# Four products of the feed-forward step's pairs 4 and 5, made at the kernel's start from the transposed input

## The chip, the cores and the metric

One core of a Trainium2 chip runs the whole block. TensorE (PE) multiplies, VectorE (DVE), ScalarE (ACT) and GpSimd (POOL) work element by element, SyncE (SP) issues most loads and stores. The metric is device time in microseconds, the median of several executions.

## The reference

```python
h = h + 0.5 * swiglu(rms_norm(h, ffn1_norm[l]), ffn1_w1[l], ffn1_w3[l], ffn1_w2[l])
...
def swiglu(x, w1, w3, w2):
    return (jax.nn.silu(x @ w1) * (x @ w3)) @ w2
```

The change lies in the first of these lines, the block's first step, with 1024 tokens of 1024 features, 2816 hidden features, all float32. `rms_norm` scales each token by one number and each feature by its gain. Attention, pooling, a merge and a second such step follow.

## The kernel before

Every float32 product is made of three products of a high and a low part (`three`), accumulated in PSUM. The matrix x is cut into 2 x 2 blocks of 512 tokens by 512 features, and a pair j of two 128-wide slices of hidden features (2j and 2j+1) is made with seven block products instead of eight, for w1 (`A`) and for w3 (`B`). `ORDER` is their order; product 1 is block b11 of x by weight block a11, product 2 is b21 by a12, added in the same bank. One product is 12 matmuls of 128x512. `Pair.a_out` and `Pair.b_out` take each bank apart: product 1 is copied as u2, product 2 is read from the bank where 1 + 2 stand, the others are added.

`begin_up1` is the kernel's start, written by hand in the order in which each engine gets its instructions; each engine works through its own queue in that order. It loads eight blocks of 128 token rows (`load_rows`, L882), between them the first weights (L76), from SyncE's queue. ScalarE squares a row block with a sum (L274), VectorE and GpSimd make the inverse root (L278, L279), VectorE scales by it and by the gain (L285), TensorE turns the block (L407, four transposes), ScalarE rounds the turned block to the high part (L408), VectorE subtracts for the low part (L411), ScalarE keeps the turned block (L415). The gain as a row is made by spreading the gain's column over 128 columns (L920), turning it (L926) and copying it from PSUM (L942, L960). `keep_on` (L916) puts filler matmuls of ones into TensorE's queue. `entry` makes products 1 and 2 of pairs 0 to 2 one after the other (`operand`: weights split at L319 and L322; `product`: L331; `out`: L567 and L591) while the later row blocks are being turned. Its first four use b11 and are products 1 of pairs 0 and 1; the fifth is product 2 of pair 0 and needs all four row blocks of b21. After that `up` runs the rest of the pairs; pairs 3 to 9 do so one after the other, all products of `A`, then all of `B`. Weights come through seven buffers (`raw`), a pair's first rows lie in one of three (`tmp`).

## Time and profile before

| | us |
|---|---|
| median of 3 executions | 1892.59 |
| lowest, highest | 1892.32, 1893.02 |
| profiled execution: its time | 1892.07 |
| profiled execution: its span on the core | 1890.2 |

A row of the timeline gives start, duration, engine, line, operation and tiles (numbers left out), the count of merged instructions, and in brackets the idle time before with what ended it. A row of stretches gives busy time and the number of instructions of each engine, then the granted clock, the share of the transfer engines and GB/s. "PEld" is TensorE's loading of weights, which overlaps with its matmuls.

### The profile page before, as it was taken

The numbers are of one execution on the slowest core, as the hardware profiler recorded it, in microseconds if no ns is written. First come the engines' busy times: TensorE is split into PE (matmuls) and PEld (weight loads), VectorE is DVE, ScalarE is ACT, GpSimd is POOL, SyncE is SP. The second block draws the span as 40 slices with busy tenths as digits, with TensorE's granted clock in tenths as the row PEclk, the third lists the DMA queues.
The fourth block names the chain that finished last, engine by engine and source line by source line (L and its number), as shares of the span: only waits on it lengthen the run. The fifth ranks groups of instructions, "written<-read, shape, count | busy, mean of one in ns | idle before, by whom it ended". The sixth has DMA issues, their size and how long they took to land.

```text
span 1890.2 us, 24694 instructions
## 1 busy us (share of the span) xinstructions
PE 1879.9 (99%) x8822; PEld 1561.9 (83%) x8822; DVE 1331.9 (70%) x1975; ACT 772.8 (41%) x1394; POOL 712.2 (38%) x533
## 2 busy tenths in 40 slices
PE   9999999999999999999999999999999999999998
PEld 8888888888888888888888888888888888888887
DVE  6776556657786777557885896887665566577867
ACT  7323333333334553334445772363333323334344
POOL 5433333331223254444555357543333333312221
PEclk9999999999999999999999999999999999999999
DMA  5154223436566526765668968744332223454654
GB/s 191 60 198 166 84 89 106 139 111 216 170 224 210 183 84 210 236 219 188 224 236 314 322 224 289 270 153 149 140 127 103 84 102 118 137 189 162 226 197 145
DMA packets 144019, 330.79 MB, mean 175 GB/s; under 512 B 17560, under 2 KB 39064, under 8 KB 142360
## 3 DMA queue, kind: packets, MB, share of 16 engines
q1 hardware_dynamic: 140152, 318.36, 48.6%
q10 hardware_dynamic: 3744, 10.85, 1.6%
q8 instruction: 70, 1.15, 0.3%
q14 instruction: 53, 0.43, 0.1%
HBM read 229.61 MB, written 99.55 MB: 174 GB/s over the span
## 4 chain that ended last, share of the span: by engine, by line
PE 57%; DVE 2%; ACT 1%; DMA 1%; issue 0%; POOL 0%; ACTq 0%; DVEq 0%; SPq 0%
PE u_mixm L331 15%; PE d_f L815 11%; PE wo L2028 4%; PE yp L1770 1%; PE u_f20b L331 1%; PE u_f21a L331 1%; PE u_f210b L331 1%; PE u_f210a L331 1%; PE u_f29b L331 1%; PE u_f29a L331 1%; PE u_f28a L331 1%; PE u_f27b L331 1%; PE u_f27a L331 1%; PE u_f26b L331 1%; PE u_f26a L331 1%; PE u_f25b L331 1%
## 5 line engine op out<-in xcount | busy, mean ns | idle before, releaser
L815 PE MATMUL d_f<-bhi_f,ahi_f 128*128 128x512 f32 x616 | 240.2, 390 | 0.0
L815 PE MATMUL d_f<-bhi_f,alo_f 128*128 128x512 f32 x616 | 239.7, 389 | 0.0
L815 PE MATMUL d_f<-blo_f,ahi_f 128*128 128x512 f32 x616 | 239.6, 389 | 0.0
L772 POOL TENSOR_TENSOR alo_f<-g_f,ahi_f 128x512 fp32r<-128x512 f32 x60 | 85.9, 1448 | 270.0 <-ACT ahi_f L768 270.0
L331 PE MATMUL u_mixm<-xhi_t_mix,wc_mixm 128*128 128x512 f32 x608 | 157.3, 391 | 0.1
L815 PEld LDWEIGHTS d_f<-bhi_f,ahi_f 128*128 128x128 f32 x616 | 115.7, 188 | 24.2 <-ACT h L415 0.5
L815 PEld LDWEIGHTS d_f<-bhi_f,alo_f 128*128 128x128 f32 x616 | 115.6, 188 | 24.2
L815 PEld LDWEIGHTS d_f<-blo_f,ahi_f 128*128 128x128 f32 x616 | 115.7, 188 | 23.7
L331 PEld LDWEIGHTS u_mixm<-xhi_t_mix,wc_mixm 128*128 128x128 f32 x608 | 113.5, 188 | 23.9 <-ACT wc_mixm L319 0.7
L331 PE MATMUL u_mixm<-xhi_b_mix,wc_mixm 128*128 128x512 f32 x456 | 120.4, 391 | 0.0
L322 POOL TENSOR_TENSOR wc_mixm<-s_mixm,wc_mixm 128x512 fp32r<-128x512 f32 x52 | 76.6, 1475 | 104.9 <-ACT wc_mixm L319 94.0
L331 PEld LDWEIGHTS u_mixm<-xhi_b_mix,wc_mixm 128*128 128x128 f32 x456 | 84.9, 188 | 17.3
L319 ACT ACTIVATE wc_mixm<-s_mixm 128x512 fp32r<-128x512 f32 x76 | 47.0, 628 | 109.4 <-DVE s_mixm L373 54.6
L768 ACT ACTIVATE ahi_f<-g_f 128x1024 fp32r<-128x1024 f32 x84 | 81.9, 975 | 3.1 <-DMA g_f<-gs_f 2.0
L331 PE MATMUL u_mixm<-xlo_t_mix,wc_mixm 128*128 128x512 f32 x304 | 81.3, 389 | 0.0
L322 POOL TENSOR_TENSOR wc_mixm<-raw,wc_mixm 128x512 fp32r<-128x512 f32 x40 | 60.2, 1505 | 40.8 <-ACT wc_mixm L319 32.4
L2028 PE MATMUL wo<-w_o,o_hi 128*128 128x512 f32 x224 | 69.3, 390 | 0.0
L768 ACT ACTIVATE bhi_f<-s_f2w 128x512 fp32r<-128x512 f32 x55 | 33.0, 628 | 86.3 <-DVE s_f2w L790 67.6
L768 ACT ACTIVATE bhi_f<-s_f1w 128x512 fp32r<-128x512 f32 x55 | 33.1, 629 | 83.4 <-DVE s_f1w L790 70.2
L331 PEld LDWEIGHTS u_mixm<-xlo_t_mix,wc_mixm 128*128 128x128 f32 x304 | 57.1, 188 | 12.0
L772 DVE TENSOR_TENSOR alo_f<-g_f,ahi_f 128x1024 fp32r<-128x1024 f32 (+1 forms) x48 | 57.6, 1200 | 7.6 <-ACT ahi_f L768 7.5
L331 PE MATMUL u_mixm<-xlo_b_mix,wc_mixm 128*128 128x512 f32 x228 | 61.0, 389 | 0.0
(1332 smaller groups left out, 4751.9 us busy)
## 6 DMA issues: line engine op xcount, KB each, us to landing
g_f<-gs_f SPq DMA_DIRECT2D x70, 512.0 KB
gs_f<-y_f SPq DMA_DIRECT2D x88, 256.0 KB
raw<-in_w2a_dram SPq DMA_DIRECT2D x35, 512.0 KB
raw<-in_w2b_dram SPq DMA_DIRECT2D x35, 512.0 KB
gs_f<-gb_f SPq DMA_DIRECT2D x46, 256.0 KB
raw<-in_w1a_dram SPq DMA_DIRECT2D x22, 512.0 KB
raw<-in_w3a_dram SPq DMA_DIRECT2D x22, 512.0 KB
raw<-in_w1b_dram SPq DMA_DIRECT2D x22, 512.0 KB
```

The source lines that it names most:

```text
L319: ac.activation(w[:, 0], src, AF.Copy)
L322: eng.tensor_tensor(w[:, 1], src, w[:, 0].bitcast(F32), op=OP.subtract)
L331: pe.matmul(p, a, b, start=(start and n == 0), stop=(n == 11), skip_group_check=not start)
L768: ac.activation(hi[:, c], src, AF.Copy)
L772: eng.tensor_tensor(lo[:, d], src[:, o], hi[:, d].bitcast(F32), op=OP.subtract)
L815: pe.matmul(self.banks[m][t], l, r, start=(first and q == 0), stop=(last and q == 2))
L1770: pe.matmul(p, a, b, start=(j == 0), stop=(j == 11))
L2028: pe.matmul(banks[m][t], l, r, start=(st == 0 and j == 0 and q == 0), stop=(st == 1 and j == 1 and q == 2))
```

## The change

Products 1 of pairs 4 and 5, for w1 and w3, are made in `begin_up1`, before x is normalised. The transposed input `x_t` (an input that both kernels have) holds b11 unscaled; four of its 128-feature slices are multiplied by the gain, which is a factor of each partition there, and split (`led_high`, `led_low`) into the space of t4. The four weight blocks are loaded (`weight`) and split (`led_split`, `led_rest`), the first two in halves. `led_run` issues the matmuls, partly for half of the slices at a time. The factor of each token, a column of the result, comes later: `means` is the row of the four inverse roots, turned from a column read with a zero step, and `led_scaled` multiplies the kept products by it and stores them to `led_dram`. In pairs 4 and 5 `fetch_a` and `fetch_b` load them as u2, product 1 is left out, and product 2 is added to u2 by VectorE.

The gain's row is turned in the same way without a spread copy; `first_scaled` reads it from PSUM. The fillers of TensorE are 7 and 2 now. Block 1's high part is made by VectorE. The fourth block of b21 is turned after the third product.

On TensorE, from the gain's transposes to the first product of pair 0 (`idle` are the fillers, `x_b11_0` to `x_b11_3` the four row blocks, `f10a1` is product 1 of pair 0), before:

```order
L926 MATMUL gain0_230<-ident_70,columns_143 128x128 x4
L926 MATMUL gain1_235<-ident_70,columns_143 128x128 x4
L916 MATMUL idle_211<-ones_71 128x128 x2
L407 MATMUL x_b11_0_252<-ident_70,x0_133 128x128 x4
L916 MATMUL idle_211<-ones_71 128x128 x2
L407 MATMUL x_b11_1_261<-ident_70,x1_134 128x128 x4
L916 MATMUL idle_211<-ones_71 128x128 x2
L407 MATMUL x_b11_2_277<-ident_70,x2_135 128x128 x4
L916 MATMUL idle_211<-ones_71 128x128 x3
L407 MATMUL x_b11_3_287<-ident_70,x3_136 128x128 x4
L916 MATMUL idle_211<-ones_71 128x128 x2
L331 MATMUL u_f10a1_300<-xhi_b11_f1_123,wc_f10a1_273 128x512 x8
```

and now, from block 0 to just before the same place (`led2` and `led3` are products 1 of pair 5; those of pair 4, `led0` and `led1`, stand ahead):

```order
L409 MATMUL x_b11_0_321<-ident_70,x0_133 128x128 x4
L1025 MATMUL u_led2_308<-xhi_t4_f1_119,wc_led2_299 128x512 x4
L1025 MATMUL u_led3_336<-xhi_t4_f1_119,wc_led3_317 128x512 x4
L409 MATMUL x_b11_1_343<-ident_70,x1_134 128x128 x4
L1025 MATMUL u_led3_336<-xlo_t4_f1_120,wc_led3_317 128x512 x4
L409 MATMUL x_b11_2_357<-ident_70,x2_135 128x128 x4
L1025 MATMUL u_led3_336<-xhi_t4_f1_119,wc_led3_317 128x512 x2
L409 MATMUL x_b11_3_369<-ident_70,x3_136 128x128 x4
L971 MATMUL means_375<-ident_70,nst_0_295 128x128
L971 MATMUL means_375<-ident_70,nst_1_302 128x128
L971 MATMUL means_375<-ident_70,nst_2_327 128x128
L971 MATMUL means_375<-ident_70,nst_3_341 128x128
```

All fillers between the blocks are gone, and the blocks' transposes stand between the new matmuls; the row after these is two more of `led3`, and then `f10a1`.

On ScalarE, from the weights of the fourth product to the weights of the fifth (`wc_f10a2`), before:

```order
L319 ACTIVATE wc_f11b1_354<-raw3_203 128x512
L408 ACTIVATE xhi_b21_f1_127<-x_b21_2_361 128x4x128
L408 ACTIVATE xhi_b21_f1_127<-x_b21_3_368 128x4x128
L591 ACTIVATE u_f102_389<-u_f10b1_336 128x512
L274 ACTIVATE columns_143,nst_5_391<-x5_138 128x1024
L415 ACTIVATE x0_133<-x_b21_0_323 128x512
L415 ACTIVATE x1_134<-x_b21_1_330 128x512
L415 ACTIVATE x2_135<-x_b21_2_361 128x512
L415 ACTIVATE x3_136<-x_b21_3_368 128x512
L319 ACTIVATE wc_f10a2_411<-raw0_195 128x512
```

and now:

```order
L320 ACTIVATE wc_f11b1_444<-raw3_216 128x512
L411 ACTIVATE xhi_b21_f1_127<-x_b21_2_451 128x4x128
L611 ACTIVATE u_f102_473<-u_f10b1_426 128x512
L411 ACTIVATE xhi_b21_f1_127<-x_b21_3_475 128x4x128
L274 ACTIVATE square2_146,nst_5_481<-x5_138 128x1024
L420 ACTIVATE x0_133<-x_b21_0_413 128x512
L420 ACTIVATE x1_134<-x_b21_1_420 128x512
L420 ACTIVATE x2_135<-x_b21_2_451 128x512
L420 ACTIVATE x3_136<-x_b21_3_475 128x512
L320 ACTIVATE wc_f10a2_501<-raw0_208 128x512
```

The fourth block's high part now follows the copy of the second product, and on TensorE its transposes have moved behind the third product:

```order
L409 MATMUL x_b21_2_451<-ident_70,x2_135 128x128 x4
L332 MATMUL u_f11a1_460<-xhi_b11_f1_123,wc_f11a1_441 128x512 x4
L332 MATMUL u_f11a1_460<-xlo_b11_f1_124,wc_f11a1_441 128x512 x4
L332 MATMUL u_f11a1_460<-xhi_b11_f1_123,wc_f11a1_441 128x512 x4
L409 MATMUL x_b21_3_475<-ident_70,x3_136 128x128 x4
L332 MATMUL u_f11b1_488<-xhi_b11_f1_123,wc_f11b1_444 128x512 x4
L332 MATMUL u_f11b1_488<-xlo_b11_f1_124,wc_f11b1_444 128x512 x4
L332 MATMUL u_f11b1_488<-xhi_b11_f1_123,wc_f11b1_444 128x512 x4
L332 MATMUL u_f10a1_385<-xhi_b21_f1_127,wc_f10a2_501 128x512 x4
```

On VectorE the scaling of block 2 (`x2_135`) stands behind the high part of block 1 and the low part of block 0:

```order
L986 SCALAR_TENSOR_TENSOR x1_134<-x1_134,nst_1_302,gain0_242 128x512
L278 TENSOR_SCALAR nst_2_327<-nst_2_327 128x1
L413 CAST xhi_b11_f1_123<-x_b11_1_343 128x4x128
L416 TENSOR_TENSOR xlo_b11_f1_124<-x_b11_0_321,xhi_b11_f1_123 128x4x128
L986 SCALAR_TENSOR_TENSOR x2_135<-x2_135,nst_2_327,gain0_242 128x512
L278 TENSOR_SCALAR nst_3_341<-nst_3_341 128x1
L986 SCALAR_TENSOR_TENSOR x3_136<-x3_136,nst_3_341,gain0_242 128x512
```

Before, it stood right behind the two small rows `nst_2` and `nst_3`.

The diff:

```diff
             x = {1: "b11", 2: "b21", 3: "b22", 4: "t4", 5: "t1", 6: "t2", 7: "t3"}[m]
             key = {1: "x", 2: "x", 5: "v", 3: "v"}.get(m, m)
-            if m not in (2, 3):
+            first = key not in self.bank
+            if first:
                 self.bank[key] = bank("mm" if key in ("x", "v") else "acc", f"u_{self.sv.name}{n}{m}")
-            self.sv.product(self.bank[key], w, x, start=m not in (2, 3))
+            self.sv.product(self.bank[key], w, x, start=first)
             if m == 3 and back:
                 raws.back(2)
             return self.bank[key]
...
+        def __init__(self, X, what, src, t, tag="acc", p=None, eng=ac):
             q = t % 4
             self.hi, self.lo = (v[:, :, q * P:(q + 1) * P] for v in X[what])
             p = self.flat = bank(tag, f"x_{what}_{t}") if p is None else p
             self.p = p.rearrange("p (k q) -> p k q", k=4)
             for k in range(4):
                 pe.transpose(self.p[:, k, :], src[:, k * P:(k + 1) * P], ident)
-            ac.activation(self.hi, self.p, AF.Copy)
+            if eng is ac:
+                ac.activation(self.hi, self.p, AF.Copy)
+            else:
+                eng.tensor_copy(self.hi, self.p)
...
+            self.led = sv.led.get(j)
+            self.order = ORDER if self.led is None else (2, *(m for m in ORDER if m not in (1, 2)))
...
+        def fetch_a(self):
+            if self.led is not None:
+                nc.sync.dma_start(self.place(0, slice(HALF, S)), self.led[0])
+
+        def fetch_b(self):
+            if self.led is not None:
+                self.u[2] = self.u2(f"{self.j}2")
+                nc.sync.dma_start(self.u[2], self.led[1])
...
             elif m == 2:
-                ac.activation(self.place(0, lows), p, AF.Silu)
+                c = self.place(0, lows)
+                if self.led is not None:
+                    ve.tensor_tensor(c, p, u2, op=OP.add)
+                    p = c
+                ac.activation(c, p, AF.Silu)
...
             q, then = then or Pair(sv, j, sums), None
-            for m in ORDER:
+            for m in q.order[:3]:
+                q.a(m)
+            q.fetch_b()
+            for m in q.order[3:]:
                 q.a(m)
             if j == NPAIR - 2:
                 between()
-            for m in ORDER[:-2]:
+            if j + 1 in sv.led:
+                then = Pair(sv, j + 1, sums)
+                then.fetch_a()
+            for m in q.order[:-2]:
                 q.b(m)
             if j == NPAIR - 2:
                 end = Pair(sv, NPAIR - 1, sums)
                 for m in ORDER[:2]:
                     end.A.operand(m)
-            for m in ORDER[-2:]:
+            for m in q.order[-2:]:
...
-    square = row("square")
-    columns_tile = tmp("columns")
-    columns = columns_tile.rearrange("p (k c) -> p k c", k=KT)
+    led_x, led_in = [], []
+    for n in range(2):
+        led_x.append(row(f"led_x{n}").rearrange("p (k c) -> p k c", k=2))
+        led_in.append(row(f"led_w{n}").rearrange("p (k c) -> p k c", k=2))
+    square = X["t1"][0][:, 0:2, :].rearrange("p k c -> p (k c)")
+    square2 = tmp("square2")
+
+    LED = (4, 5)
+    led_dram = [dram.tile([P, HALF], F32, name=f"led{q}") for q in range(4)]
...
     def load_all():
-        load_rows(0, 1, 2, 3)
+        def features(kk):
+            nc.sync.dma_start(led_x[kk], x_t[0, kk])
+
+        def weight(q):
+            nc.sync.dma_start(led_in[q // 2][:, q % 2], (w1a, w3a)[q % 2][2 * LED[q // 2]][:, LOWS])
+
+        features(0)
+        weight(0)
+        weight(1)
+        features(1)
+        load_rows(0)
+        weight(2)
+        load_rows(1)
+        weight(3)
+        load_rows(2, 3)
...
-        def widen(b):
-            k = slice(4 * b, 4 * b + 4)
-            ve.tensor_copy(columns[:, k], gain1[:, k, None].to_broadcast([P, 4, P]))
+        def spread(p, columns):
+            for k, c in enumerate(columns):
+                pe.transpose(p[:, k * P:(k + 1) * P], c.to_broadcast([P, P]), ident)
+            return p
 
         def gains(b):
-
-            p = bank("acc", f"gain{b}")
-            for k in range(4):
-                pe.transpose(p[:, k * P:(k + 1) * P], columns[:, 4 * b + k], ident)
-            return p
+            return spread(bank("acc", f"gain{b}"), [gain1[:, k:k + 1] for k in range(4 * b, 4 * b + 4)])
+
+        def gain_copy(b):
+            ac.activation(gain_row[:, (LOWS, HIGHS)[b]], g[b], AF.Copy)
...
+        def first_scaled(t):
+            ve.scalar_tensor_tensor(h[t][:, LOWS], h[t][:, LOWS], inv[t][:, 1:2], g[0], op0=OP.mult, op1=OP.mult)
+
+        xhi, xlo = X["t4"]
+        kept = [sv1.half_tile("s", f"led{q}") for q in range(4)]
+        means = sv1.half_tile("u", "means")
+        led_w, led_p = {}, {}
...
+        def led_high(k, eng=ac):
+            if eng is ac:
+                ac.activation(xhi[:, k], led_x[k // 2][:, k % 2], AF.Copy, scale=gain1[:, k:k + 1])
+            else:
+                ve.tensor_scalar(xhi[:, k], led_x[k // 2][:, k % 2], gain1[:, k:k + 1], None, op0=OP.mult)
+
+        def led_low(k):
+            ve.scalar_tensor_tensor(xlo[:, k], led_x[k // 2][:, k % 2], gain1[:, k:k + 1], xhi[:, k].bitcast(F32),
+                                    op0=OP.mult, op1=OP.subtract)
+
+        def led_split(q, c):
+            if q not in led_w:
+                led_w[q] = fp.tile([P, 2, HALF], F32R, tag="wc", bufs=4, name=f"wc_led{q}")
+            w, src = led_w[q], led_in[q // 2][:, q % 2]
+            ac.activation(w[:, 0, c], src[:, c], AF.Copy)
+
+        def led_rest(q, c):
+            w, src = led_w[q], led_in[q // 2][:, q % 2]
+            gp.tensor_tensor(w[:, 1, c], src[:, c], w[:, 0, c].bitcast(F32), op=OP.subtract)
+
+        FRONT, BACK, WHOLE = slice(0, 2 * P), slice(2 * P, HALF), slice(0, HALF)
+        count = {}
+
+        def led_run(q, ks, terms):
+            w = led_w[q]
+            if q not in led_p:
+                led_p[q] = bank("mm", f"u_led{q}")
+                count[q] = 0
+            for i in terms:
+                for k in ks:
+                    r = slice(k * P, (k + 1) * P)
+                    a, b = three((w[:, 0, r], w[:, 1, r]), (xhi[:, k, :], xlo[:, k, :]))[i]
+                    pe.matmul(led_p[q], a, b, start=count[q] == 0, stop=count[q] == 11)
+                    count[q] += 1
+
+        def led_scaled(q):
+            ve.tensor_tensor(kept[q], kept[q] if q < 2 else led_p[q], means, op=OP.mult)
+            nc.sync.dma_start(led_dram[q], kept[q])
+            sv1.led.setdefault(LED[q // 2], [None, None])[q % 2] = led_dram[q]
...
+        keep_on(7)
+        g = {}
+        for b in (1, 0):
+            g[b] = gains(b)
+        keep_on(2)
+        led_high(0)
+        led_high(1, ve)
+        led_split(0, FRONT)
+        led_split(0, BACK)
+        led_rest(0, FRONT)
+        led_low(0)
+        led_low(1)
+        led_rest(0, BACK)
+        led_split(1, FRONT)
+        led_rest(1, FRONT)
+        led_split(1, BACK)
+        led_rest(1, BACK)
+        led_run(0, (0, 1), (0, 1, 2))
+        led_run(1, (0, 1), (0, 1))
+        led_run(1, (0, 1), (2,))
+        gain_copy(0)
+        led_high(2)
+        led_high(3, ve)
+        led_low(2)
+        led_low(3)
+        led_run(0, (2, 3), (0, 2, 1))
+        led_run(1, (2, 3), (0, 2, 1))
+        gain_copy(1)
         squares(0, square)
-        widen(1)
         inverse(0)
-        g = [gains(b) for b in range(2)]
-        keep_on(2)
-        ve.tensor_copy(gain_row[:, LOWS], g[0])
-        for t in range(1, 4):
-            squares(t, square)
+        led_split(2, WHOLE)
+        led_rest(2, WHOLE)
+        squares(1, square)
+        ve.tensor_copy(kept[0], led_p[0])
+        first_scaled(0)
         inverse(1)
+        led_run(2, range(4), (0, 1))
+        led_split(3, WHOLE)
+        led_rest(3, WHOLE)
+        ve.tensor_copy(kept[1], led_p[1])
         rows(0, "b11", LOWS)
-        keep_on(2)
-        rows(1, "b11", LOWS)
+        squares(2, square)
+        led_run(2, range(4), (2,))
+        first_scaled(1)
         inverse(2)
+        led_run(3, range(4), (0,))
+        squares(3, square)
+        rows(1, "b11", LOWS, "acc", ve)
+        r[0].lower()
+        first_scaled(2)
         inverse(3)
-        keep_on(2)
         pairs = [Pair(sv1, j, sums, True, j == 2) for j in range(3)]
         entry = pre_run(sv1, [(q, m) for m in (1, 2) for q in pairs[:2]] + [(pairs[2], m) for m in (1, 2)],
                         pairs[0], h[:4])
+        led_run(3, range(4), (1,))
+        rows(2, "b11", LOWS)
         entry.operand(0)
-        rows(2, "b11", LOWS)
-        keep_on(3)
+        led_run(3, (0, 1), (2,))
+        first_scaled(3)
         rows(3, "b11", LOWS, "mm")
-        keep_on(2)
-        ac.activation(gain_row[:, HIGHS], g[1], AF.Copy)
-        for t in range(4):
+        p = spread(bank("acc", "means"), [inv[t][:, 1:2] for t in range(4)])
+        led_run(3, (2, 3), (2,))
+        for t in range(1, 4):
             r[t].lower()
         sv1.terms = (0, 2, 1)
         entry.product(0)
         sv1.terms = (0, 1, 2)
+        ac.activation(means, p, AF.Copy)
         entry.operand(1)
+        for q in (2, 3):
+            led_scaled(q)
         for t in range(4):
             r[t].keep(h[t][:, LOWS])
 
-        square2 = columns_tile
         squares(4, square2)
         for t in (0, 1):
+            scaled_part(t, HIGHS, gain_row)
             rows(t, "b21", HIGHS)
         entry.product(1)
         entry.out(0)
         entry.operand(3)
         inverse(4)
         r[0].lower()
-        for t in (2, 3):
-            rows(t, "b21", HIGHS)
-        for t in (1, 2):
-            r[t].lower()
+        scaled_part(2, HIGHS, gain_row)
+        rows(2, "b21", HIGHS)
+        r[1].lower()
+        scaled_part(3, HIGHS, gain_row)
+        r[2].lower()
         entry.product(2)
         entry.out(1)
+        rows(3, "b21", HIGHS)
         squares(5, square2)
         r[3].lower()
         for t in range(4):
         entry.out(2)
         entry.operand(5)
         entry.out(3)
+        for q in (0, 1):
+            led_scaled(q)
```

More of the change, by code (lines that the diff above doesn't have):

```diff
@@ L312, in __init__ @@
             self.terms = (0, 1, 2)
+            self.led = {}
         def half_tile(self, tag, n):
@@ L398, in tile_block @@
     class Rows:
-        def __init__(self, X, what, src, t, tag="acc", p=None):
+        def __init__(self, X, what, src, t, tag="acc", p=None, eng=ac):
             q = t % 4
@@ L595, in b_out @@
                 c = self.place(0, lows)
+                if self.led is not None:
+                    u[3] = self.sv.half_tile("u", f"{j}3")
+                    ve.tensor_tensor(u[3], p, u[2], op=OP.add)
+                    p = u[3]
                 ve.tensor_tensor(c, p, c, op=OP.mult)
             elif m == 7:
-                u[3] = self.sv.half_tile("u", f"{j}3")
+                if 3 not in u:
+                    u[3] = self.sv.half_tile("u", f"{j}3")
                 ve.tensor_tensor(u[3], p, u[2], op=OP.add)
@@ L929, in begin_up1, with rows @@
+        def gain_copy(b):
+            ac.activation(gain_row[:, (LOWS, HIGHS)[b]], g[b], AF.Copy)
         r = {}
-        def rows(t, what, c, tag="acc"):
-            scaled_part(t, c, gain_row)
-            r[t] = Rows(X, what, h[t][:, c], t, tag)
-        keep_on(12)
-        widen(0)
+        def rows(t, what, c, tag="acc", eng=ac):
+            r[t] = Rows(X, what, h[t][:, c], t, tag, eng=eng)
+        def first_scaled(t):
+            ve.scalar_tensor_tensor(h[t][:, LOWS], h[t][:, LOWS], inv[t][:, 1:2], g[0], op0=OP.mult, op1=OP.mult)
```

## The prediction

> **What bounds the kernel now.** I read the page first, then a table of stretches, then the timeline of the first 27 us. The page says that TensorE is the bound:
>
> ```profile
> span 1890.2 us, 24694 instructions
> ...
> PE 1879.9 (99%) x8822; PEld 1561.9 (83%) x8822; DVE 1331.9 (70%) x1975; ACT 772.8 (41%) x1394; POOL 712.2 (38%) x533
> ```
>
> The next table has, for pairs 3, 4 and 5 of the first feed-forward step (one row each), the busy time of each engine:
>
> ```profile
> core 0: us, PE busy (x) PEld busy (x) DVE busy (x) ACT busy (x) POOL busy (x), PEclk, DMA share, GB/s
> 134.99:173.07 38.08, 38.08 (x169) 31.53 (x168) 25.53 (x35) 12.21 (x20) 13.88 (x10) 1.00 0.40 138
> 173.07:211.15 38.08, 38.08 (x169) 31.53 (x168) 22.76 (x32) 12.22 (x20) 12.49 (x9) 1.00 0.32 108
> 211.15:249.23 38.08, 38.08 (x169) 31.53 (x168) 21.52 (x32) 12.21 (x20) 12.68 (x9) 1.00 0.28 99
> ```
>
> A pair is 14 products of 12 matmuls: 38.08 / 14 = 2.72 us for a product, 0.227 for a matmul, with no gap. So a product taken out of a pair is worth 2.72 us, and one put in elsewhere costs what TensorE loses there. Only the front has time to give. These are its rows that I use (start, duration, engine, line):
>
> ```profile
> 1.05 4.93 PE L916 MATMUL idle<-ones 128*128 128x128 f32 x24 [1.05 <-DVE mhalf L198]
> ...
> 4.13 1.06 ACT L274 ACTIVATE square<-x 128x1024 f32<-128x1024 f32 x1 [0.97 <-DMA x<-in_x_dram]
> ...
> 4.31 0.76 DVE L920 COPY columns<-gain 128x512 f32<-128x512 f32 x2 [3.31 <-DMA gain<-in_ffn_norm_dram]
> ...
> 5.88 1.06 PE L926 MATMUL gain<-ident,columns 128*128 128x128 f32 x8
> ...
> 7.00 1.06 ACT L274 ACTIVATE square<-x 128x1024 f32<-128x1024 f32 x1 [0.19 <-DMA x<-in_x_dram]
> ...
> 7.36 1.41 DVE L285 SCALAR_TENSOR_TENSOR x<-x,nst,gain_ffn 128x512 f32<-128x512 f32 x2
> ...
> 8.27 1.06 ACT L274 ACTIVATE square<-x 128x1024 f32<-128x1024 f32 x1
> ...
> 8.70 0.14 DVE L278 TENSOR_SCALAR nst<-nst 128x1 f32<-128x1 f32 x1
> 8.91 0.55 POOL L279 TENSOR_TENSOR nst<-nst,mhalf 128x1 f32<-128x1 f32 x1 [0.98 <-DVE nst L278]
> 8.99 0.47 PEld L407 LDWEIGHTS x_b<-ident,x 128*128 128x128 f32 x4
> ...
> 10.99 1.62 POOL L322 TENSOR_TENSOR wc_f10a<-raw,wc_f10a 128x512 fp32r<-128x512 f32 x1 [0.30 <-ACT wc_f10a L319]
> ...
> 11.40 2.48 DVE L411 TENSOR_TENSOR xlo_b_f<-x_b,xhi_b_f 128x512 fp32r<-128x512 f32 x4
> ...
> 12.23 0.60 ACT L408 ACTIVATE xhi_b_f<-x_b 128x512 fp32r<-128x512 f32 x1 [0.58 <-PE x_b L407]
> ...
> 12.88 2.14 PE L331 MATMUL u_f10a<-xhi_b_f,wc_f10a 128*128 128x512 f32 x8 [0.24 <-ACT xhi_b_f L408]
> ```
>
> The first product starts at 12.88, on the chain load, square, power, scaling, transpose, high part. Until then TensorE does fillers and 24 transposes. That is the time which the change wants to use.
>
> **What leaves.** Four products, 4 x 2.72 = **-10.88 us** in pairs 4 and 5. They then take 32.64 us each. VectorE keeps up: it loses no work that matters and gains two additions from PSUM (0.69 each, below), so some 23 of 32.64 us. ScalarE and GpSimd lose work there. The fetched products are asked for at least three products (8 us) before they are used, one 256 KB load each.
>
> **When the first ordinary product now starts.** TensorE's queue ahead of it holds 14 filler matmuls, 8 transposes for the gains, 4 fillers, the 48 new matmuls and 5 x 4 transposes. The gains wait for the vector and the identity matrix. The vector landed by 4.31; the columns were written at 5.07, yet the transposes began at 5.88, so the identity matrix came last, about 5.8. Behind smaller loads it may come sooner; bounds are 4.3 (beside the vector) and 5.9; I take 5.2. Eight transposes (0.9) and the fillers (0.45) put the first new matmul at 6.55. Its inputs: features at about 4.3 (where the first 512 KB landed before), high part 0.63, two lower parts at 0.71 to 0.75: 6.5, in time.
>
> The new matmuls run while the loads saturate the memory. There a product takes longer, as these rows show (12 matmuls each; the loads run at 408 and 411 GB/s, then stop):
>
> ```profile
> core 0: us, PE busy (x) PEld busy (x), PEclk, DMA share, GB/s
> 12.87:15.77 2.90, 2.89 (x12) 2.18 (x12) 1.00 1.02 408
> 16.75:19.59 2.84, 2.83 (x12) 2.16 (x12) 1.00 1.03 411
> 23.19:25.92 2.73, 2.73 (x13) 2.25 (x12) 1.00 0.00 0
> ```
>
> So 0.235 us for a matmul. The 32 ahead of the first row block's transposes end at 6.55 + 7.52 = 14.1. Can the other engines feed them? From 4.3 on, ScalarE has two scaled copies (0.6), four half splits (about 0.4 each, a half of 0.63 with its fixed part; bounds 0.3 and 0.63), two gain copies, two squares (1.25 with the read-out) and two splits: 7.8 us, done at 12.1. VectorE has two scaled copies (not in the trace; between 0.38, as one of the column copies, and 0.75, as a scaling), four lower parts, two copies out (0.7) and two scalings: 7.6 at most. GpSimd has four half subtractions (0.8), two whole ones (1.6) and two powers after 5.4: 7.5. All are ahead of 14.1. The loads too: 3.5 MB stand ahead of the third row block's end; 512 KB took (7.00 - 4.13) / 2, less waiting some 1.3 us, so it lands at about 12 and is squared after 15.
>
> From there it is a chain of handovers. Transposes of block 0 end at 14.5. ScalarE: high part (0.53), square of block 2 (1.25): 16.4. VectorE 0.14 and GpSimd 0.55: 17.15. But VectorE has work in front of the scaling: block 1 is turned only after eight more matmuls, at 16.85, and its high part is now on VectorE (0.69), then block 0's lower part (0.62): 18.2. Scaling 0.71: 18.9. TensorE had run dry at 17.8: **1.2 us of waiting**. The same ring once more for block 3: 0.14, 0.55, 0.75, so 20.4 instead of 19.9: **0.55**. Four transposes, the means' four (0.45 each) and two matmuls: the first product starts at **21.8**, 8.9 later than 12.88. Without the two waits it would be 20.0. Front: -10.88 + 8.9 = **-2.0 us**; with the identity matrix at 4.3 it is -2.9, at 5.9 -1.3.
>
> **What it runs into next.** After the first product ScalarE and TensorE go on as before, shifted, up to one place: the transposes of the fourth high row block stand behind the third product now, not ahead of it. What hangs on them in ScalarE's queue:
>
> ```profile
> 20.23 1.09 ACT L408 ACTIVATE xhi_b_f<-x_b 128x512 fp32r<-128x512 f32 x2 [0.92 <-PE x_b L407]
> ...
> 21.20 0.61 ACT L591 ACTIVATE u_f<-u_f10b 128x512 f32<-128x512 f32 x1
> ...
> 21.68 1.07 ACT L274 ACTIVATE columns<-x 128x1024 f32<-128x1024 f32 x1
> ...
> 22.72 2.07 ACT L415 ACTIVATE x<-x_b 128x512 f32<-128x512 f32 x4
> ...
> 24.63 0.68 ACT L319 ACTIVATE wc_f10a<-raw 128x512 fp32r<-128x512 f32 x1
> ...
> 25.93 1.07 PE L331 MATMUL u_f10a<-xhi_b_f,wc_f10a 128*128 128x512 f32 x4
> ```
>
> From the high part of that block (its start about 20.75) to the split weights of the fifth product (25.31) it is 4.55 us, less the 0.48 of the copy in between, which goes ahead now: **4.1 us**. The split was ready 0.6 us before TensorE asked at 25.93. In the change only the fourth product (2.72) stands between the transposes and the fifth, so TensorE waits 4.1 - 2.7 = **+1.4 us** (1.9, if no instruction overlaps the next; less only if ScalarE is ahead, which its in-order queue excludes). Nothing takes this back: the queue behind holds no filler.
>
> The four multiplications by the means fall on VectorE (about 0.7 each) before the row blocks 4 to 7; that is where it has room:
>
> ```profile
> 25.00:30.00 5.00, 5.00 (x30) 4.30 (x29) 0.20 (x1) 3.03 (x7) 4.62 (x4) 1.00 0.00 0
> ```
>
> (a stretch: TensorE, its weight loads, VectorE, ScalarE, GpSimd), and in the timeline
>
> ```profile
> 29.80 0.70 DVE L466 TENSOR_TENSOR x_b<-x_b,x 128x512 f32<-128x512 f32 x1 [6.15 <-PE x_b L472]
> ```
>
> VectorE was idle for 6.15 us, so 2.8 us cost nothing. GpSimd's first difference reuses the space of a kept product, whose store must be out first; at 1.3 us for 512 KB it is out some us before. 0.1 us for small things.
>
> **Sum:** -10.88 + 8.9 + 1.4 + 0.1 = **-0.5 us**. The profiled execution took 1892.07 us, 0.5 under the median of the three (1892.59); so 1891.6 there, **1892.1** as a median. Its own range, from the bounds of the identity matrix and of this wait: -1.4 to +0.7, 1891.2 to 1893.3. A measurement here tells about 0.2% (3.8 us) from no change, so this is no change.
>
> **Rivals.** *Faster: the waits do not come.* TensorE alone then sets the front, and the fifth product's split is covered: -10.88 + 7.1 = -3.8, 1888.8; with one of the two waits about -2, 1890.5. For it: ScalarE is 41% busy. Against: both are chains through queues that run in order, and the durations are measured. 0.2.
>
> *Slower: the clock.* Filler matmuls by count:
>
> ```profile
> 1.05:5.05 4.00, 4.00 (x18) 4.00 (x19) 1.00 0.80 281
> 5.30:5.85 0.55, 0.55 (x6) 0.49 (x5) 1.00 1.06 432
> ```
>
> 18 in 4.00 us, then 6 in 0.55: TensorE runs at half rate until about 5.1, after 4 us without a gap, though the granted clock reads 1.00. The change has 14 fillers, over at 1.05 + 14 x 0.213 = 4.0, then a hole until 5.2. If the hole sets the count back, full rate comes 4 us after 5.2, at 9.2, and half of those 4 us is lost: +2.0, so +1.5 in all, 1894.1; if it comes at 12, +3.4, 1895.5. It decides if the rate changes later than about 6. For it: nothing but an unbroken run is seen to raise the rate. Against: the fillers fill 3 of the 4.1 us up to 5.2. 0.27.
>
> [...]
>
> *Slower: the queue of loads.* The four fetches stand in SyncE's queue ahead of weight loads. If one waits for its buffer, the load behind it is late, and TensorE has no cover in a pair. One such wait of a product and a load's 1.3 us is 4 us; one or two of them give 1896 to 1899. For it: a pair's first row takes one of three buffers. Against: those pairs moved 99 to 108 GB/s of the 410 seen. 0.1.
>
> *It does not do what it says:* pairs 4 and 5 do not get shorter, since VectorE becomes the bound. At 23 of 32.64 us it cannot, unless its work bunches. 0.03; +9, 1901.
>
> **Chances.** Forecast 0.4, no waits 0.2, clock 0.27, loads 0.1, last 0.03. Faster by over 0.2% (under 1888.8) is the end of the first rival: 0.08. Slower by over 0.2% (over 1896.4): the last two and the end of the clock's, 0.17. Within: 0.75. The range reaches to the middle of both sides' rivals: 1889.5 to 1896.
>
> **What would show it.** In the changed profile: pairs 4 and 5 at 32.64 us; first new matmul near 6.5; the first product near 21.8, with waits of 1.2 and 0.5 of the third and fourth row blocks' transposes on VectorE; then one wait of 1.4 on ScalarE's split before the fifth product. A step between 0.47 and 0.235 us among the new matmuls would be the clock. I am wrong if the first product starts before 20.5 or after 23, or if TensorE waits anywhere after the first 70 us.

## The result and the profile after

The changed kernel takes 1896.02 us (median of 22 runs, 1893.83 to 1897.88) against 1892.66 before (22 runs, 1892.10 to 1893.15): 3.4 us more, ratio 1.0017 with a 95% interval of 1.0011 to 1.0023. The interval leaves out 1, so the changed kernel is slower, by a little less than the 0.2% that the forecast called no change. The forecast was 1892.1 with a range from 1889.5 to 1896, and the median lies 0.02 us past its end. The times of the change spread over 4 us, those of before over 1.

The profiled execution of the change took 1897.2 us, 1.2 more than the median. Its page:

```profile
span 1895.4 us, 24694 instructions
...
PE 1879.5 (99%) x8798; PEld 1560.0 (82%) x8798; DVE 1341.8 (71%) x1988; ACT 773.4 (41%) x1395; POOL 714.6 (38%) x536
```

TensorE has 24 instructions less than before (28 fillers less, four transposes more) and is busy for as long. The table of TensorE's waits says where else it stood still (waits in all, times, longest):

```profile
PE gain L971 <- DMA ident<-in_c_ident_dram: 1.8, 1, 1.8
PE x_b L409 <- DVE x L986: 1.5, 2, 1.1
PE wo L2169 <- DVE o_lo L2157: 1.4, 2, 0.7
PE u_f10a L332 <- ACT wc_f10a L320: 1.4, 1, 1.4
...
PE u_mixm L332 <- ACT wc_mixm L320: 0.7, 1, 0.7
```

Before, only `x_b` (0.8) and four of 0.3 and less stood there, apart from the start. To see what each costs, the program is cut at the same matmuls in both: first ordinary product, pair 3, first matmul of `u_mixm`, first of `yp`, first of `wo`, first product of the second feed-forward step that has `u_f20a` for its output, last matmul. Before (stretch, length, TensorE's busy time):

```profile
12.88:134.99 122.11, 122.11 (x568) 1.00 0.39 133
134.99:653.75 518.76, 518.72 (x2307) 1.00 0.45 154
653.75:1034.68 380.93, 380.79 (x1742) 1.00 0.61 210
1034.68:1156.24 121.56, 120.72 (x898) 1.00 0.80 272
1156.24:1248.89 92.65, 92.53 (x424) 1.00 0.74 277
1248.89:1883.12 634.23, 634.09 (x2821) 1.00 0.41 142
```

and the change:

```profile
24.54:148.68 124.14, 122.67 (x569) 1.00 0.35 122
148.68:656.56 507.88, 507.87 (x2259) 1.00 0.47 159
656.56:1038.02 381.46, 380.74 (x1742) 1.00 0.61 210
1038.02:1159.51 121.49, 120.68 (x898) 1.00 0.79 269
1159.51:1253.77 94.26, 92.83 (x423) 1.00 0.73 274
1253.77:1888.00 634.23, 634.10 (x2821) 1.00 0.41 142
```

Read side by side: the stretch with pairs 4 and 5 is 10.88 shorter, exactly what was counted for four products. Against this gain the first ordinary product starts 11.66 later, the entry up to pair 3 is 2.03 longer, the mixer (the stretch from `u_mixm` to `yp`) 0.53, the stretch of `wo` 1.61. With 0.3 behind the last matmul that is the 5.2 us between the spans. Pair 4 itself (pair 5 is as long):

```profile
186.76:219.40 32.64, 32.64 (x145) 27.04 (x144) 23.14 (x33) 10.13 (x16) 11.68 (x8) 1.00 0.40 137
```

TensorE has no gap there, and VectorE is at 23 of 32.64 us. The gain was real; the front did not pay for it. TensorE's rows of the front, in the change:

```profile
1.05 3.36 PE L967 MATMUL idle<-ones 128*128 128x128 f32 x14 [1.05 <-DVE mhalf L198]
6.21 1.94 PE L971 MATMUL gain<-ident,gain 128*128 128x128 f32 x8 [1.80 <-DMA ident<-in_c_ident_dram]
7.94 1.06 PE L967 MATMUL idle<-ones 128*128 128x128 f32 x4
8.65 1.20 PE L1025 MATMUL u_led<-xhi_t_f,wc_led 128*128 128x512 f32 x2
9.65 0.86 PE L1025 MATMUL u_led<-xlo_t_f,wc_led 128*128 128x512 f32 x2
10.35 1.09 PE L1025 MATMUL u_led<-xhi_t_f,wc_led 128*128 128x512 f32 x4
...
16.73 0.60 PE L409 MATMUL x_b<-ident,x 128*128 128x128 f32 x4
...
21.67 0.66 PE L409 MATMUL x_b<-ident,x 128*128 128x128 f32 x4 [1.11 <-DVE x L986]
...
23.14 0.66 PE L409 MATMUL x_b<-ident,x 128*128 128x128 f32 x4 [0.35 <-DVE x L986]
```

The identity matrix is used at 6.21, not at 5.2. The eight transposes take 1.94 instead of 1.06. The first two new matmuls take 1.00 from start to start (8.65 to 9.65), the next two 0.70, and from 10.35 on one takes 0.23: full rate comes at about 10.2, and before at about 5.2. The waits of the row blocks, 1.11 and 0.35, are the ones that were forecast (1.2 and 0.55), and so is the one of the fifth product:

```profile
38.66 0.66 ACT L320 ACTIVATE wc_f10a<-raw 128x512 fp32r<-128x512 f32 x1
...
39.37 1.21 PE L332 MATMUL u_f10a<-xhi_b_f,wc_f10a 128*128 128x512 f32 x4 [1.42 <-ACT wc_f10a L320]
```

### The profile page after: what moved, and what is told of

Read it like the earlier page. It is cut to its first block, busy times and chain, and to the rows that moved or that the text cites. A ratio compares the mean times of both kernels' runs of the same rounds, so it can differ in the third digit from the quotient of the medians.

```text
span 1895.4 us, 24694 instructions
## 1 busy us (share of the span) xinstructions
PE 1879.5 (99%) x8798; PEld 1560.0 (82%) x8798; DVE 1341.8 (71%) x1988; ACT 773.4 (41%) x1395; POOL 714.6 (38%) x536
## 4 chain that ended last, share of the span: by engine, by line
PE 54%; DVE 3%; ACT 2%; issue 1%; DMA 1%; POOL 1%; SPq 0%; ACTq 0%; DVEq 0%; POOLq 0%
PE u_mixm L332 15%; PE d_f L846 8%; PE wo L2169 4%; PE yp L1911 1%; PE u_f20b L332 1%; PE u_f21a L332 1%; PE u_f210a L332 1%; PE u_f29a L332 1%; PE u_f28a L332 1%; PE u_f25a L332 1%; PE u_f24a L332 1%; PE u_f23a L332 1%; PE u_f22a L332 1%; PE u_f27b L332 1%; PE u_f27a L332 1%
```

## The experiments

**The change again.** Nothing is edited; the question is which of these terms belong to one execution.

> The changed kernel once more, nothing edited. Theory (four terms): the profiled execution of the change stands 5.2 us of span over before; by its rows 0.8 of it is the first ordinary product (24.54 against 12.88, less 10.88), 1.4 the wait of the fifth product, 0.5 a wait in the mixer (u_mixm on ScalarE's split) and 1.45 two waits of the output projection (wo on o_lo), the rest 1.0 in small gaps. If the half rate of the front and the late waits differ between executions, a second profile shows the same 1.4 and the same waits of the row blocks (1.1 and 0.35), but another end of the half rate (10.2 in the first) or other late waits; median 1896, spread again about 4 us. Rival (all of it fixed by the order of work): every landmark within 0.2 us of the first profile, and the spread of the times comes from somewhere that no row shows.

Measured: 1895.95 us (11 runs, 1894.34 to 1897.38), ratio 1.0014 (1.0006 to 1.0023). The fifth product waits 1.4 again, the row blocks 1.1 and 0.4. The late waits are other ones: `wo` 0.2 instead of 1.4 and the mixer 0.2 instead of 0.7. The clock is another one too:

```profile
0.84:4.25 3.41, 3.20 (x14) 1.00 0.71 211
4.25:7.67 3.42, 1.42 (x14) 1.00 0.95 340
7.67:11.08 3.41, 3.41 (x11) 0.50 1.01 373
```

(stretch, length, TensorE's busy time, granted clock; the column reads 1.00 ahead of the first change on record, but the 14 fillers of the first row take 0.23 us each and the four from 7.29 on 0.09, so the first row is at half rate.) Here the rate went up at 4.25, as the fillers ended, when TensorE had been busy for 3.20 us without a gap; it went down again at 7.67, TensorE having been busy for 1.42 of the 3.42 us before, and up for good at 11.08. The gain's transposes ran at full rate (1.06) and the first new matmuls at half (two in 1.00 from 7.66). The first ordinary product came at 24.45, hardly other than 24.54. The rival that all is fixed by the order of work falls.

**24 fillers, as before the change.**

```diff
-        keep_on(7)
+        keep_on(12)
         g = {}
```

> 24 filler matmuls ahead of the gain's transposes, as before the change, instead of 14. Clock theory: the fillers reach to the landing of the identity matrix (6.15), full rate comes near 5.2 as before, the 8 transposes take 0.9 instead of 1.94 and the first new matmul starts at 7.3 to 7.6 instead of 8.65; the half rate of the first four new matmuls (0.75) is gone too: first ordinary product near 22.6 instead of 24.54, median 1894.0, and the spread of the times shrinks below 2 us. Rival (late loads make the time): the front shortens but median and spread stay at 1896 and 4 us. Rival (the chain through the row blocks sets the front, not TensorE): first ordinary product stays at 24.3 or later, waits of the row blocks grow by 1.5 to 2.

Measured: 1893.88 us (1893.27 to 1894.48), ratio to before 1.0004 (0.9995 to 1.0013), and 2.1 us less than the change run beside it. The spread is 1.2. In the profile:

```profile
6.36 1.06 PE L971 MATMUL gain<-ident,gain 128*128 128x128 f32 x8
...
7.62 0.71 PE L1025 MATMUL u_led<-xhi_t_f,wc_led 128*128 128x512 f32 x2
8.17 0.62 PE L1025 MATMUL u_led<-xlo_t_f,wc_led 128*128 128x512 f32 x2
...
22.79 2.05 PE L332 MATMUL u_f10a<-xhi_b_f,wc_f10a 128*128 128x512 f32 x8
```

The identity matrix is not earlier (transposes at 6.36), but everything behind it is at full rate: the first ordinary product at 22.79, 1.75 earlier. The clock theory holds, and most of the spread goes with the half rate (3.0 in the 11 runs of the change beside it). Both rivals fall: the median and the spread shrink, and the waits of the row blocks stay at 1.1 and 0.4. What is left over the forecast of 21.8 is 1.0, about as much as the gain's transposes are later than assumed (6.36 against 5.2).

**The kept products in scratch tensors that exist already.** In before no late wait of the mixer stood in the table, and four new tensors had moved the addresses of all later ones.

```diff
-    led_dram = [dram.tile([P, HALF], F32, name=f"led{q}") for q in range(4)]
+    led_dram = [late_w[1 + q // 2][:, q % 2, :HALF] for q in range(4)]
```

> The four kept products are stored into parts of scratch tensors that exist already (used again only much later), so the scratch memory is laid out as before the change. Placement theory: the four new tensors shift all scratch tensors behind them, transfers of the mixer and of the merge collide in another way, and that made the waits of 0.5 (u_mixm) and 1.45 (wo): both gone or at before's 0 and 0.3, 1.9 us less, median 1894.1. Rival (those waits come with the later start or by chance): median 1896 as the change, and the same kind of wait at about the same places.

Measured: 1896.14 us, ratio 1.0018 (1.0009 to 1.0027): no gain. In its waits the mixer has 0.7 and `wo` 0.7:

```profile
PE u_mixm L332 <- ACT wc_mixm L320: 0.7, 1, 0.7
PE wo L2169 <- DVE o_lo L2157: 0.7, 1, 0.7
```

The placement theory falls: the mixer's wait comes without the four new tensors too. The run gave the latest full rate of all instead. Two stretches of its front:

```profile
5.54:8.95 3.41, 2.60 (x13) 1.00 0.98 374
8.95:12.36 3.41, 3.41 (x10) 1.00 1.03 394
```

From 6.34 on, when the identity matrix was there, TensorE was busy without a gap, but at half rate until 12.36: two new matmuls take 1.00 from 8.79, and 0.48 from 12.35. The first ordinary product came at 25.66.

**The square of row block 5 behind the fifth product's split.**

```diff
-        squares(5, square2)
         r[3].lower()
...
         entry.operand(4)
+        squares(5, square2)
         entry.out(2)
```

> The square of row block 5 moved in ScalarE's queue from ahead of the four kept differences to behind the split of the fifth product. Theory of the prediction (ScalarE's in-order queue between the fourth high part and the split sets the wait): the wait of the fifth product falls from 1.42 by the square and its read-out (1.24) to about 0.2, and the time by 1.2 to 1894.8. Rival (the split waits for a buffer or a load): wait stays at 1.4. Rival (given back later): the wait goes, and a later one of the same size appears before 70 us, since the square is now late for the fifth row block; median 1896.

Measured: 1895.85 us, ratio 1.0014 (1.0005 to 1.0022), no different from the change. The profile:

```profile
38.04 1.20 PE L332 MATMUL u_f10a<-xhi_b_f,wc_f10a 128*128 128x512 f32 x4 [0.38 <-ACT wc_f10a L320]
...
42.69 0.66 PE L409 MATMUL x_t<-ident,s_f1t 128*128 128x128 f32 x4 [0.72 <-POOL s_f1t L461]
```

The wait fell from 1.42 to 0.38, as ScalarE's queue says, and 0.72 came back at the next place: with the square behind the first split, ScalarE makes the second split 1.3 us after the fifth product's start (0.3 in the change), GpSimd's part of it is late by 0.8, and its difference `s_f1t` stands behind that in its queue. The last rival was right: given back. First product to pair 3 took 123.88, 0.26 less than in the change.

**The fourth row block early** (on 24 fillers, so that the clock does not blur it).

```diff
         rows(2, "b21", HIGHS)
-        r[1].lower()
         scaled_part(3, HIGHS, gain_row)
+        rows(3, "b21", HIGHS)
+        r[1].lower()
         r[2].lower()
         entry.product(2)
         entry.out(1)
-        rows(3, "b21", HIGHS)
```

> 24 fillers, and the fourth row block of b21 scaled and turned ahead of the third product again, as before the change. Against the run with 24 fillers alone (1893.88; first ordinary product at 22.79, pair 3 at 146.96, that is 124.17 between them where before has 122.11). Theory (the wait of the fifth product is the price of this place in the order, through ScalarE's queue): no wait of the fifth product, 122.1 to 122.4 between the two landmarks, 1891.9 to 1892.2. Rival (VectorE is late with the scaling of block 3, two multiplications by the means being ahead of it): TensorE waits 0.5 to 0.75 ahead of the third product, gain 1.2 at most. Rival (as when the square was moved: GpSimd's difference is late next): the wait goes and 0.7 comes back at x_t, gain 0.3, 1893.6.

Measured: 1891.98 us (1891.50 to 1892.42), ratio 0.9993 (0.9983 to 1.0002), 1.9 less than with 24 fillers alone. The entry from the first ordinary product to pair 3, with 24 fillers and then with this edit too:

```profile
22.79:146.96 124.17, 122.68 (x569) 101.05 (x569) 96.64 (x137) 56.54 (x103) 54.68 (x43) 1.00 0.37 127
```

```profile
22.47:144.69 122.22, 122.17 (x570) 101.19 (x569) 94.99 (x137) 56.55 (x103) 55.02 (x43) 1.00 0.37 130
```

122.22 is what before has (122.11). No wait of the fifth product, none on VectorE, none at `x_t`: the place of four transposes, with the scaling ahead of them, costs 1.95 us, and both rivals fall. This one edit and the fillers take the change from 3.4 over before to 1 us under it (an interval that reaches to no change).

**The scaling of block 2 early** (on 24 fillers).

```diff
         squares(3, square)
-        rows(1, "b11", LOWS, "acc", ve)
-        r[0].lower()
         first_scaled(2)
         inverse(3)
+        rows(1, "b11", LOWS, "acc", ve)
...
-        for t in range(1, 4):
+        for t in range(4):
             r[t].lower()
```

> 24 fillers, and on VectorE the scaling of block 2 (with the first step of block 3's power) ahead of block 1's high part and block 0's lower part. Against 24 fillers alone (block 2's transposes wait 1.27 and start at 19.91, block 3's wait 0.52 and start at 21.39, first ordinary product 22.79). Theory (VectorE's two pieces of work, 0.69 and 0.62 with their wait for block 1's transposes, make the first wait): block 2 near 18.9, block 3 near 20.4, first ordinary product 21.7 to 21.9, 1892.9. Rival (the power's chain or the square of block 2 sets it): starts stay within 0.3. Rival (block 0's lower part is late then): the first product gets a gap of 0.3 to 0.7 ahead of its last four matmuls.

Measured: 1892.81 us (1892.17 to 1893.53), ratio 0.9999 (0.9990 to 1.0008), 1.07 less than with 24 fillers alone. The intervals of the two runs overlap, so the landmarks must carry it. The third and fourth row block and the first product:

```profile
18.98 0.66 PE L409 MATMUL x_b<-ident,x 128*128 128x128 f32 x4
...
20.45 0.66 PE L409 MATMUL x_b<-ident,x 128*128 128x128 f32 x4 [0.36 <-DVE x L986]
...
21.84 2.06 PE L332 MATMUL u_f10a<-xhi_b_f,wc_f10a 128*128 128x512 f32 x8
```

The first ordinary product comes 0.95 earlier, as the theory says: the wait of 1.1 is gone, so it was VectorE's queue. The second wait (0.36) stays.

**The identity matrix first** (14 fillers).

```diff
-    nc.scalar.dma_start(ident, c_ident)
...
+        nc.sync.dma_start(ident, c_ident)
         features(0)
```

> The change with 14 fillers as it is, the identity matrix loaded first on SyncE's queue, ahead of the features, instead of second on ScalarE's. Against the change (identity used at 6.2 to 6.4, first ordinary product 24.25 to 25.66 in four profiles, 1896.0). Theory (the hole of the fillers comes from the late identity matrix, and the late full rate from the hole): the gain's transposes start at 4.5 with the gain's vector, the hole is 0.3 instead of 2.1, full rate comes before 7.7, first ordinary product 22.0 to 23.0, 1893.0 to 1894.0, spread under 2. Rival (the matrix is late because all loads share the 16 DMA engines): it lands after 5.5 again, 1896. Rival (features or weights that land after it now bound the new matmuls): gains early, but TensorE waits 1 to 2 us for the second half of the features (8.5 before), first ordinary product 23.5 or later.

Measured: 1894.3 us (1893.68 to 1894.90 in ten of the eleven runs), ratio 1.0006 (0.9997 to 1.0015). The transposes start at 4.20, the hole is nearly gone and full rate comes at 5.9:

```profile
4.20 1.89 PE L971 MATMUL gain<-ident,gain 128*128 128x128 f32 x8
5.90 0.63 PE L967 MATMUL idle<-ones 128*128 128x128 f32 x4
6.33 0.73 PE L1025 MATMUL u_led<-xhi_t_f,wc_led 128*128 128x512 f32 x2
```

The first new matmul comes 1.3 earlier than with 24 fillers, and the first ordinary product later (22.95 against 22.79), since TensorE then waits: 0.64 for a lower part of the features, since VectorE's first two took 1.90 us instead of 1.42 in the change, with no load named as a wait, and shorter behind it, since VectorE gets the second half of the features at 9.32 instead of 8.35. So the theory holds for the clock, and the last rival in part, with shorter waits than it said: behind an early identity matrix the other loads come later. Fillers do as well and are simpler.

**Both edits of order, then two more steps.** The first has both edits above and 24 fillers; the second also takes the square of row block 2 ahead of block 0's high part; the third also leaves out the 4 fillers behind the gain's transposes.

```diff
+        squares(2, square)
         rows(0, "b11", LOWS)
-        squares(2, square)
```

```diff
             g[b] = gains(b)
-        keep_on(2)
         led_high(0)
```

> 24 fillers with both edits of order, the fourth row block of b21 early and the scaling of block 2 early. If the two gains are independent: first ordinary product 21.8, pair 3 at 144.0, 1890.9 to 1891.2, faster than before (1892.7) by 1.5 and more. If they share a bound (VectorE before the fourth row block): 1891.5 to 1892.

> The kernel with 24 fillers and both edits of order (1891.08), and the square of row block 2 ahead of the high part of block 0 in ScalarE's queue. Theory (what is left of the row blocks' waits, 0.26 and 0.52, is the chain square, power, scaling, and ScalarE stands idle for 3.4 us ahead of block 0's high part): both waits gone, first ordinary product 21.2 instead of 21.96, 1890.3. Rival (row block 2 lands late, and the square blocks the high part behind it): no gain, or a wait of the first product on block 0's parts.

> As the one before, and without the 4 fillers between the gain's transposes and the first new matmul. If the inputs are there (lower part of the features at 6.7, front half of the first weights at 6.5 in the run with the fourth row block early), the new matmuls start 0.45 earlier: first ordinary product 20.7 to 20.8, 1889.9. Rival (the loads set the pace of the new matmuls: second half of the features lands at 8.2 to 8.5): the 0.45 comes back as a wait ahead of the second half, 1890.3.

Measured: 1891.08 (ratio 0.9989, 0.9980 to 0.9998), 1890.10 (0.9986, 0.9977 to 0.9995) and 1890.45 us (0.9985, 0.9977 to 0.9994). The two orders add up. The square gives 1.0 where 0.8 was expected; the row blocks do not wait any more, so the second wait was the chain from the square of its row block:

```profile
18.62 0.60 PE L409 MATMUL x_b<-ident,x 128*128 128x128 f32 x4
18.98 0.71 PE L1025 MATMUL u_led<-xhi_t_f,wc_led 128*128 128x512 f32 x2
19.53 0.60 PE L409 MATMUL x_b<-ident,x 128*128 128x128 f32 x4
```

The last step was a miss: no gain that can be told, and a spread of 2.3 us (1889.14 to 1891.40). The second is 2.8 us under the runs of before beside it (1892.88) and 5.9 under the change: the idea pays, if only 2.8 of the 10.88 us, with the work put in the right places.

**The kernel before with 14 fillers, and once more as it was.**

```diff
-        keep_on(12)
+        keep_on(7)
         widen(0)
```

> The kernel before the change with 14 filler matmuls ahead of the gain's transposes instead of 24, nothing else. [...] Rival (fillers have no bearing on the rate): full rate at 5.2 to 6, 12.88, 1892.7.

> The kernel before, for a second profile of it. If the late waits of the change (0.2 to 0.85 in the mixer in nine profiles, 0.28 to 1.75 at wo) are chance of the transfers in each execution, this one may show up to 0.85 in the mixer too, instead of 0.19. If they come with the change, it shows 0.19 and 0.28 again. The time is near 1892.7 in either case.

Measured: 1892.5 us (1891.7 to 1894.38, ratio 1.0000, 0.9991 to 1.0009) with 14 fillers, 1893.04 in one run as it was. With 14, the transposes of the gain and of block 0 run at half rate here too, and only block 1's do not:

```profile
5.99 1.94 PE L926 MATMUL gain<-ident,columns 128*128 128x128 f32 x8 [1.58 <-DMA ident<-in_c_ident_dram]
...
8.73 1.11 PE L407 MATMUL x_b<-ident,x 128*128 128x128 f32 x4
...
10.15 0.60 PE L407 MATMUL x_b<-ident,x 128*128 128x128 f32 x4
```

So full rate does not come at 5.2 to 6, and the rival falls; but the time is not longer than that of before beside it (1892.88). The first product starts at 13.43. So the hole that costs the change 2 us costs before nothing that can be told. The second profile of before starts its first product at 13.83 instead of 12.88 (the third row block was squared at 7.95 instead of 7.00, after a wait for its load), so 1 us of the front is chance there, and the 13.43 lies between the two. In neither profile does TensorE wait in the mixer.

## Why the prediction was wrong

- **What leaves (-10.88).** Right to the hundredth: 518.76 against 507.88, pairs of 32.64. The rival that VectorE becomes the bound is out, and so is the one of the fetches: TensorE has no gap from 60 to 700 us.
- **The front (-2.0).** This is the step that failed, in "the eight transposes (0.9) and the fillers (0.45) put the first new matmul at 6.55". It came at 8.65. 1.0 of the 2.1 is the identity matrix (6.21, bounds 4.3 to 5.9): I took smaller loads ahead for an earlier landing. The trace keeps sixteen marks of the parts in which this load lands. In the change half of them stand by 5.21, near the 5.2 that I took, but the last at 6.07; before, all stand between 5.51 and 5.75. The transposes begin 0.13 after the last mark in both. So most of the load did come sooner, and its last parts came later; why these lag is open. In the ten profiles of changed kernels in which its load keeps its place the transposes begin at 6.05 to 6.55, and at 5.88 and 5.99 in the two of before where TensorE stood ready. 1.1 is the half rate in the transposes and fillers.

  From there to block 0's transposes it took 8.08 instead of 7.55: about 0.75 more for four new matmuls at half rate, less a little, since the others took some 0.228 and not 0.235. The loads were no reason to take 0.235: from 13.55 to 16.73 they ran at 417 GB/s, and a new matmul took 0.227. From block 0 to the first ordinary product 7.81 instead of 7.7: both waits on VectorE came (1.11 and 0.35). For the first, the run with the scaling early shows that the reason was right; the second goes only when the square is earlier too. So the front was +0.8 and not -2.0, and the first ordinary product, at 24.54, came after the 23 that I had named as a sign of being wrong.
- **The clock.** I had it as a rival at 0.27, with a loss of 2.0 to 3.4 us and 1894.1 to 1895.5, and it should have been the forecast: 24 fillers against 14 showed 2.1 us. "The fillers fill 3 of the 4.1 us up to 5.2" was the wrong argument: with the hole of 2 us behind them, full rate came for good at 9.4, 10.2, 11.1 and 12.4 in the four profiles of the change's front with 14 fillers, and in one of these it had come at 4.25 and gone again at 7.67. An unbroken run of some 4 us, on which I had reckoned, does not tell the time either: TensorE had been busy without a gap for 3.96 us when the rate went up at 10.2, and for 6.02 at 12.36. No run shows a rule that gives the 12 us behind my loss of 3.4; what the runs show is these four times, which differ between executions of the same front. With 24 fillers the spread fell from 3 us to 1.2.
- **What it runs into next (+1.4).** The wait was 1.42, for the reason given. Its price was 2.0, as the entry's 122.11 against 124.14 and the run with the fourth block early (1.95) show: the rest is TensorE's start behind the wait and the product after it. The term was mis-sized by 0.5 (0.1 was set down for small things).
- **Waits after 70 us.** I said I would be wrong if there were any. The profiled execution has 2.1 us of them; the other ten profiles of changed kernels show that `wo`'s part is chance of this execution: 0.3 or less in eight of them, 0.7 and 0.8 in two. With the other terms (front about 0.8 to 1, entry 2.0) the median's 3.4 leaves some 0.4 to 0.6 for them and for what follows the last matmul. That is rough: the first ordinary product starts between 24.25 and 25.66 in the four profiles of the change's front with 14 fillers, and the first product of before at 12.88 or 13.83.
- **Open.** The mixer's wait is 0.7 to 0.8 in seven profiles of the changed kernels and 0.2 to 0.3 in four, and absent or under 0.2 in three of the kernel before. VectorE waits there for a load of what was just stored (`ro`; 6.5 us in three waits in the change). It also comes without the four new tensors; what it does come from was not tried.

## What to carry to other kernels

Work that is moved into a part where an engine was idle makes that engine the bound there, and what was free becomes dear: before, 10 fillers less cost nothing that can be told; with real matmuls behind it the same hole costs 2 us and a spread of 3 to 4. So read the rate from the distance of TensorE's starts up to the first real product (here 0.50 us against 0.23 for a matmul of 128x512), and keep the fillers until the input that it waits for has really landed, with the landing of its last part taken from a row and not from the size of what is ahead. And when four transposes are moved behind a product, follow every queue that hangs on them, the next engine's too: taking 1.24 us out of ScalarE's queue gave 0.3, putting the transposes back gave all of 1.95.

## What the runs showed that I had not expected

- The clock goes both ways within 11 us: full from 4.25, half from 7.67, full from 11.08 in one execution. How long TensorE was busy without a gap before the rate went up differs: 3.20 us at 4.25 there, 3.96 in the first profile of the change, 6.02 in the run with the scratch tensors. In the run with the square moved it was 3.11, with full rate from about 9.4:

```profile
6.00:9.41 3.41, 3.11 (x14) 1.00 0.98 370
```

  What decides when the rate changes was not shown.

- The column of the granted clock reads 1.00 until the first change on record, also where matmuls of a kind stand at twice their distance: the stretch from 6.21 to 10.17 of the change reads 1.00, and two new matmuls take 1.00 us there, against 0.46 from 11.28 on. The distance of their starts is the safe reading.
- 64 KB of identity matrix, asked for at 1.2 us on a queue with nothing else but the gain's vector, were used at 6.05 to 6.55 us while the other queue's loads ran. Put first on that other queue, they were used at 4.20, when the fillers ended, with no wait for them in the table.
